# A PEER decoder block: expert gates written once to device memory as a table, instead of made anew for every chunk of expert rows

## The chip, the core and the metric

The kernel runs on one core of a Trainium2 chip. The metric is the device time of one launch in microseconds (us). Its engines appear in the rows as PE (TensorE), PEld (TensorE's weight loads), DVE (VectorE), ACT (ScalarE), POOL (GpSimd) and SP (SyncE, which here only issues transfers).

## What is computed

A decoder block over 256 tokens of width 2048: a token mixer (sparse attention and pooling), then a retrieval over 16384 single-neuron experts, which is the part that the change touches. Each token has 8 heads; each head picks 16 experts, and an expert's number is a pair of keys, first and second, each of 128. The reference, cut to this part:

```python
s_top, i_top = lax.top_k(sub, PEER_TOPK)
cand = s_top[..., 0, :, None] + s_top[..., 1, None, :]
cand_idx = i_top[..., 0, :, None] * PEER_KEYS + i_top[..., 1, None, :]
...
best, pos = lax.top_k(cand, PEER_TOPK)
experts = jnp.take_along_axis(cand_idx, pos, axis=-1)
gates = jax.nn.softmax(best, axis=-1)
...
    u = peer_u[ec]
    a = jax.nn.gelu(jnp.einsum('cd,ced->ce', hc, u, ...), approximate=False)
    vv = peer_v[ec]
    return jnp.einsum('ce,ced->cd', (a * gc).astype(hc.dtype), vv)
```

The kernel doesn't gather. It computes the activations of all 16384 experts for all 256 tokens, multiplies them with a gate that is zero where a token hasn't picked the expert, and goes on through all rows of peer_v.

## The kernel before

**Rows and chunks.** The experts are 128 rows (first key) of 128 (second key, on the partitions). Four chunks of CH = 32 rows follow each other. `up(c, a, per_unit)` computes the activations of chunk c: for each of its 32 rows it loads 1 MB of peer_u into one of RAW = 4 buffers "raw" (`load`), splits each half into a rounded part wH on ScalarE (line 120) and the rest wL on VectorE (line 121), three buffers of each, and makes 48 products of 128x256 (`mm3`, lines 130 to 132: wH with hH, wH with hL, wL with hH). A row is thus two halves of 24 products, one for each wH and wL. ScalarE's gelu (line 741) writes the row into `a`. `down(c, a, ...)` takes `a` through peer_v in the same way. The order is up(0), up(1), down(0), down(1), up(2), up(3), down(2), down(3).

**Gates.** For a token, the 128 picks give a first key, a second key and a gate. The picks stand on the partitions, so the gates of a token are a product over its picks: second-key mask (128 picks x 128 keys, "o2") with first-key mask times gate ("o1", in two 16-bit parts q = 0 and 1). `g_pieces(a, c)` does this for the 32 first keys of chunk c alone: `gates_piece` makes the first-key masks of 32 tokens (lines 705 and 708), `mult_piece` the second-key masks of 2 x 8 tokens (line 717) and 32 products of 32 columns into a PSUM tile "gp" (line 722), and scales and multiplies them into `a` (line 726). This gives 512 products of 32 columns per chunk, and the second-key masks of all 256 tokens anew in each chunk.

**Order.** The small pieces stand in a list `side`; `run_side(n)` takes n of them. `step` takes one behind every row of up and every pair of rows of down. `pace(R_U)` puts in a reduction for the modulation (`ada`, line 136, with a load of its own into a raw buffer) behind every fourth row while some are left. In up(0) the side pieces are the top-16 searches and the decoding of both 128-token groups ("routing"); in up(1) the gates of chunk 0, in down(0) those of chunk 1, in up(3) and down(2) those of chunks 2 and 3. Each engine then works in a fixed order of its own, which the framework's scheduler makes; a buffer that is taken again waits for all who used it. "o1" of q = 0 has one buffer, of q = 1 two, "o2" two, "gp" two. All loads are issued by SP, in order.

Of the kernel before, what the change touches and what calls it, by code (L numbers as in the profile page):

```python
# [9 lines left out]
F32 = mybir.dt.float32  # L10
F32R = mybir.dt.float32r
F16 = mybir.dt.float16
U32 = mybir.dt.uint32
AF = mybir.ActivationFunctionType
ALU = mybir.AluOpType
# [4 lines left out]
P = 128  # L20
T = 256
D = 2048
# [6 lines left out]
CH = 32  # L29
KGROUPS = ((0, 4), (4, 10), (10, 16))  # L30
NGU = 43
RAW = 4
R_K, R_Y, R_GA, R_WO, R_PQ, R_U = 0.6, 0.4, 0.7, 0.6, 0.3, 0.25
TB = 8
GATE_SCALE = 2.0 ** 15


@with_exitstack
def kernel(
# [22 lines left out]
    nc = tc.nc  # L62
    wgrp_in = (wgrp0_in, wgrp1_in, wgrp2_in)
    dve, act, pe = nc.vector, nc.scalar, nc.tensor
# [3 lines left out]
    stream = ctx.enter_context(tc.tile_pool(name="stream", bufs=3))  # L68
# [96 lines left out]
    def run_side(n):  # L165
        for _ in range(n):
            if side:
                side.pop(0)()
# [462 lines left out]
    def top_list(t, h):  # L631
        for s in range(2):
            l = 2 * h + s
            top16(stop_[t][:, l], itop[t][:, l], sub[l][:, t])

    def top_cand(t, h):
        l = 2 * h
        cand = px.tile([P, 16, 16], F32, name="cand", bufs=1)
        dve.tensor_tensor(cand, stop_[t][:, l, :, None].to_broadcast([P, 16, 16]),
                          stop_[t][:, l + 1, None, :].to_broadcast([P, 16, 16]), ALU.add)  # L640
        top16(best[:, h], pos[:, h], cand.rearrange("p a b -> p (a b)"))
# [24 lines left out]
    def decode_flip(t, s):  # L666
        ps = gps.tile([P, 512], F32, name="gp")[:, :P]
        pe.transpose(ps, late["sel", t, s], ident)
        act.copy(idxT[s][:, P * t:P * t + P], ps)

    def gates_of(t):
        e = px.tile([P, 8, 16], F32, name="cand", bufs=1)
        sm = px.tile([P, 8, 2], F32, name="gsm", bufs=2)
        dve.tensor_tensor(e, best, best[:, :, 0:1].to_broadcast([P, 8, 16]), ALU.subtract)
        act.activation(e, e, AF.Exp)
        dve.tensor_reduce(sm[:, :, 0:1], e, axis=AX.X, op=ALU.add)
        dve.reciprocal(sm[:, :, 1:2], sm[:, :, 0:1])
        dve.tensor_tensor(e, e, sm[:, :, 1:2].to_broadcast([P, 8, 16]), ALU.mult)
        late["e", t] = e
# [8 lines left out]
    def new_a(c):  # L688
        if c % 2 == 0:
            return [px.tile([P, ND, T], F32, name=f"r{i}") for i in (2, 3)]  # L690
        return [main.tile([P, ND, T], F32, name="r1"), px.tile([P, ND, T], F32, name="r4")]

    def g_pieces(a, c):
        o1_of = {}

        def gates_piece(grp):
            t0 = 32 * grp
            o1 = [px.tile([P, 32 // TB, CH, TB], F16, name=f"o1{q}", bufs=1 + q) for q in range(2)]
            o1_of[grp] = o1

            def per_token(src):
                return (src[:, t0:t0 + 32].rearrange("p (g t) -> p g t", t=TB)[:, :, None, :]
                        .to_broadcast([P, 32 // TB, CH, TB]))

            dve.tensor_tensor(o1[1], iota2[:, None, CH * c:CH * c + CH, :].to_broadcast([P, 32 // TB, CH, TB]),
                              per_token(idxT[0]), ALU.is_equal)
            for q in range(2):
                dve.tensor_tensor(o1[q], o1[1], per_token(gT[q]), ALU.mult)

        def mult_piece(b):  # L710
            t0 = 16 * b
            o1 = o1_of[b // 2]
            ps = gps.tile([P, 512], F32, name="gp")
            for x in range(16 // TB):
                t1 = t0 + TB * x
                o2 = px.tile([P, P, TB], F16, name="o2", bufs=2)
                dve.tensor_tensor(o2, iota2, idxT[1][:, None, t1:t1 + TB].to_broadcast([P, P, TB]), ALU.is_equal)  # L717
                g = (t1 % 32) // TB
                for i in range(TB):
                    k = CH * (TB * x + i)  # L720
                    for q in range(2):
                        pe.matmul(ps[:, k:k + CH], o2[:, :, i], o1[q][:, g, :, i], start=q == 0, stop=q == 1)  # L722
            v = ps.rearrange("p (t i) -> p i t", i=CH)
            for k in range(2):
                av = a[k][:, :, t0:t0 + 16]
                dve.scalar_tensor_tensor(av, v[:, 16 * k:16 * k + 16], 1.0 / GATE_SCALE, av,  # L726
                                         op0=ALU.mult, op1=ALU.mult)

        out = []
        for grp in range(8):  # L730
            out.append(lambda grp=grp: gates_piece(grp))
            out += [lambda b=b: mult_piece(b) for b in (2 * grp, 2 * grp + 1)]
        return out

    def up(c, a, per_unit):
        for e in range(CH):
# [32 lines left out]
                    k = 8 * hf + j - 1  # L769
                    nc.sync.dma_start(out=out[:, k:k + 2, :], in_=xT[:, k:k + 2, :])  # L770

    for t in range(2):
        for h in range(8):
            if t:
                side.append(lambda t=t, h=h: top_list(t, h))
            side.append(lambda t=t, h=h: top_cand(t, h))
        side.append(lambda t=t: decode(t, 0))
        side.append(lambda t=t: (decode_flip(t, 0), decode(t, 1)))
        side.append(lambda t=t: (decode_flip(t, 1), gates_of(t)))
        side.append(lambda t=t: gates_flip(t))  # L780

    def step(e):
        run_side(1)
        pace(R_U)

    a0 = new_a(0)
# [100 lines left out]
```

## Time and profile before

| | |
|---|---|
| three runs | 2384.88, 2385.82 (median), 2390.25 us |
| span of the profiled execution, first to last instruction | 2378.8 us |
| the median beyond that span | 7.0 us |
| PE, DVE, ACT busy, share of the span | 98%, 69%, 42% |
| up(0), first to last gelu | 771.23 to 962.16 us |
| up(1) | 966.56 to 1177.61 us |
| up(2) | 1581.04 to 1759.60 us |
| up(3) | 1765.36 to 1976.40 us |

The profiled execution's own time is its span; what a run takes beyond it lies before the first and after the last instruction. Busy shares are means over the whole; what bounds a stage is read in that stage, from the rests of its busiest engine and from what ended them.

### The profile page before, as it was taken

Reading aid. Unit: us, or ns where it says so; the run is one execution under the profiler, and the core shown is the slowest. Engines: PE = TensorE matmul, PEld = TensorE weight load, DVE = VectorE, ACT = ScalarE, POOL = GpSimd, SP = SyncE. Lnnn points to the kernel's source line nnn. Section 1 sums busy time; section 2 is a strip of 40 time slices with the busy share of each in tenths; the row PEclk is TensorE's granted clock in tenths of the full one; section 3 lists DMA queues with packets and bytes.
Section 4 is the critical chain, followed back from the end, with each engine's and each line's share of the span. In section 5 each row is a group of like instructions: output and inputs, shape, how many; then the busy total and the mean of one; then the engine's idle time right before and its main releaser. Section 6 shows DMA issues by size and latency. Waiting matters only on the chain.

```text
span 2378.8 us, 46564 instructions
## 1 busy us (share of the span) xinstructions
PE 2329.5 (98%) x19824; PEld 2288.2 (96%) x19824; DVE 1639.2 (69%) x2611; ACT 1002.9 (42%) x1479; POOL 4.8 (0%) x11
## 2 busy tenths in 40 slices
PE   6999999999999999999999999999999999999999
PEld 5899988999899899999999999999999999999999
DVE  7888977688777997665577655554445656675555
ACT  4544433744344343433433444444433333334443
POOL 0000000000000000000000000000000000000000
PEclk8999999999999999999999999999999999999999
DMA  8988866688755466544544455555554444445563
GB/s 341 333 312 315 312 232 234 247 322 303 291 188 205 178 237 224 207 167 145 176 151 150 160 179 177 195 188 185 179 177 146 156 160 160 144 158 169 187 201 119
DMA packets 88049, 494.04 MB, mean 208 GB/s; under 512 B 7913, under 2 KB 8961, under 8 KB 49441
## 3 DMA queue, kind: packets, MB, share of 16 engines
q1 hardware_dynamic: 87698, 490.90, 58.3%
q8 instruction: 155, 2.54, 0.4%
q14 instruction: 52, 0.43, 0.0%
q0 software_dynamic: 144, 0.17, 0.0%
HBM read 488.93 MB, written 2.11 MB: 206 GB/s over the span
## 4 chain that ended last, share of the span: by engine, by line
PE 87%; DVE 7%; DMA 4%; issue 1%; ACT 1%; SPq 0%; DVEq 0%; ACTq 0%
PE acc L130 26%; PE acc L132 26%; PE acc L131 26%; PE gp L722 5%; DMA raw<-in_ada_dram 3%; PE acc L503 2%; DVE wL L121 2%; DVE raw L136 2%; DVE o L660 1%; ACT wH L120 0%; PE mps L593 0%; DMA raw<-in_wgrp_dram 0%; PE mps L549 0%; PE mps L407 0%; PE mps L393 0%
## 5 line engine op out<-in xcount | busy, mean ns | idle before, releaser
L120 ACT CAST wH<-raw 128x1024 fp32r<-128x1024 f32 (+2 forms) x738 | 753.3, 1022 | 1229.0 <-PE acc L131 1167.3
L121 DVE TENSOR_TENSOR wL<-raw,wH 128x1024 fp32r<-128x1024 f32 (+2 forms) x738 | 874.3, 1188 | 526.8 <-ACT wH L120 525.4
L130 PE MATMUL acc<-hH,wH 128*128 128x256 f32 x3248 | 928.2, 286 | 19.7 <-ACT wH L120 18.2
L132 PE MATMUL acc<-hH,wL 128*128 128x256 f32 x3248 | 921.1, 284 | 6.1 <-DVE wL L121 5.9
L131 PE MATMUL acc<-hL,wH 128*128 128x256 f32 x3248 | 921.9, 284 | 0.1
L130 PEld LDWEIGHTS acc<-hH,wH 128*128 128x128 f32 x3248 | 626.7, 193 | 23.9 <-ACT wH L120 21.1
L132 PEld LDWEIGHTS acc<-hH,wL 128*128 128x128 f32 x3248 | 624.7, 193 | 9.2 <-DVE wL L121 9.0
L131 PEld LDWEIGHTS acc<-hL,wH 128*128 128x128 f32 x3248 | 626.1, 193 | 0.7 <-DVE hL L567 0.3
L130 PE MATMUL acc<-aH,wH 128*128 128x256 f32 x2048 | 577.4, 283 | 0.0
L132 PE MATMUL acc<-aH,wL 128*128 128x256 f32 x2048 | 576.8, 282 | 0.0
L131 PE MATMUL acc<-aL,wH 128*128 128x256 f32 x2048 | 576.6, 282 | 0.0
L130 PEld LDWEIGHTS acc<-aH,wH 128*128 128x128 f32 x2048 | 386.1, 189 | 0.0
L132 PEld LDWEIGHTS acc<-aH,wL 128*128 128x128 f32 x2048 | 385.9, 188 | 0.0
L131 PEld LDWEIGHTS acc<-aL,wH 128*128 128x128 f32 x2048 | 385.8, 188 | 0.0
L136 DVE CUSTOM_DVE_ANT_0 raw<-raw,cb 128x2048 f32<-128x2048 f32 x96 | 219.5, 2287 | 24.4 <-DMA raw<-in_ada_dram 24.2
L717 DVE TENSOR_TENSOR o<-iota,idxT 128x1024 f16<-128x1024 f16 x128 | 88.0, 688 | 92.4 <-PE gp L722 92.4
L722 PE MATMUL gp<-o,o 128*128 128x32 f16 x2048 | 137.7, 239 | 0.0
L722 PEld LDWEIGHTS <-o 128*128 128x128 f16 x2048 | 129.5, 163 | 2.9
L759 DVE TENSOR_TENSOR aL<-r,aH 128x256 fp32r<-128x256 f32 x256 | 107.0, 419 | 0.0
L758 ACT CAST aH<-r 128x256 fp32r<-128x256 f32 x256 | 102.2, 401 | 2.4 <-DVE r L726 2.4
L131 PE MATMUL acc<-m,wH 128*128 128x256 f32 x256 | 71.9, 282 | 0.0
L726 DVE SCALAR_TENSOR_TENSOR r<-gp,r 128x256 f32<-128x256 f32 x128 | 48.4, 420 | 21.5 <-PE gp L722 21.5
(207 smaller groups left out, 1397.5 us busy)
## 6 DMA issues: line engine op xcount, KB each, us to landing
raw<-in_u_dram SPq DMA_DIRECT2D x128, 1024.0 KB, 4.8
raw<-in_v_dram SPq DMA_DIRECT2D x128, 1024.0 KB, 5.1
raw<-in_ada_dram SPq DMA_DIRECT2D x96, 1024.0 KB, 5.5
raw<-in_wgrp_dram SPq DMA_DIRECT2D x43, 768.0 KB, 6.0
raw<-in_ybr_dram SPq DMA_DIRECT2D x16, 1024.0 KB, 6.0
raw<-in_wga_dram SPq DMA_DIRECT2D x16, 1024.0 KB, 4.9
raw<-in_wout_dram SPq DMA_DIRECT2D x16, 1024.0 KB, 4.8
raw<-in_wpq_dram SPq DMA_DIRECT2D x16, 1024.0 KB, 6.2
```

Source lines behind the costliest of these rows:

```text
L120: act.copy(wH[:, :n], src)
L121: dve.tensor_tensor(wL[:, :n], src, wH[:, :n], ALU.subtract)
L130: pe.matmul(ps, wH, xH, start=start, stop=False, **kw)
L131: pe.matmul(ps, wH, xL, start=False, stop=False, **kw)
L132: pe.matmul(ps, wL, xH, start=False, stop=stop, **kw)
L136: dve.tensor_tensor_reduce(raw, raw, cb, scale=1.0, scalar=0.0, op0=ALU.mult, op1=ALU.add, accum_out=modr[:, i:i + 1])
L503: pe.matmul(ps, ybr[0][:, o:o + P], pooled[k], start=k == 0, stop=k == 7)
L717: dve.tensor_tensor(o2, iota2, idxT[1][:, None, t1:t1 + TB].to_broadcast([P, P, TB]), ALU.is_equal)
L722: pe.matmul(ps[:, k:k + CH], o2[:, :, i], o1[q][:, g, :, i], start=q == 0, stop=q == 1)
L726: dve.scalar_tensor_tensor(av, v[:, 16 * k:16 * k + 16], 1.0 / GATE_SCALE, av, op0=ALU.mult, op1=ALU.mult)
L758: act.copy(aH, src)
L759: dve.tensor_tensor(aL, src, aH, ALU.subtract)
```

## The change

The gates of all 128 first keys are made once. `gates_build(x)`, x = 0 to 31, takes 8 tokens: both masks over all 128 keys (lines 705 and 706 of the changed kernel), two multiplications with the gate parts (708), 16 products of 128 columns (715) into two "gp" tiles, and two scalings on ScalarE (718) into "gstage", which is one of the four raw buffers. After every second build GpSimd's queue writes the stage, 1 MB, to a table "gdram" in device memory (722). The builds stand in `side` between the routing pieces, and `step` takes R_G = 1.1 pieces per row, so that they run in up(0) and up(1). `gates_apply(a, c, z)`, four per chunk, loads the chunk's 32 first keys of 64 tokens from the table (727), 1 MB in runs of 512 bytes, into a raw buffer, and multiplies `a` with them in two operations of 128x1024 (730). Lines above the change are one higher than before: wH 121, wL 122, the reduction 137.

```diff
--- before.py
+++ after.py
@@ -32,6 +32,7 @@
 RAW = 4
 R_K, R_Y, R_GA, R_WO, R_PQ, R_U = 0.6, 0.4, 0.7, 0.6, 0.3, 0.25
 TB = 8
+R_G = 1.1
 GATE_SCALE = 2.0 ** 15
 
 
@@ -690,47 +691,46 @@
             return [px.tile([P, ND, T], F32, name=f"r{i}") for i in (2, 3)]
         return [main.tile([P, ND, T], F32, name="r1"), px.tile([P, ND, T], F32, name="r4")]
 
+    gdram = dram.tile([P, 64, P, 4], F32, name="gdram")
+    gstage = {}
+
+    def gates_build(x):
+        t1 = TB * x
+        o2 = px.tile([P, P, TB], F16, name="o2", bufs=2)
+        o1 = [px.tile([P, P, TB], F16, name=f"o1{q}", bufs=1 + q) for q in range(2)]
+
+        def per_token(src):
+            return src[:, None, t1:t1 + TB].to_broadcast([P, P, TB])
+
+        dve.tensor_tensor(o2, iota2, per_token(idxT[1]), ALU.is_equal)
+        dve.tensor_tensor(o1[1], iota2, per_token(idxT[0]), ALU.is_equal)
+        for q in range(2):
+            dve.tensor_tensor(o1[q], o1[1], per_token(gT[q]), ALU.mult)
+        if x % 2 == 0:
+            gstage[0] = stream.tile([P, D], F32, name="raw", bufs=RAW)
+        for y in range(2):
+            ps = gps.tile([P, 512], F32, name="gp")
+            for i in range(4):
+                for q in range(2):
+                    pe.matmul(ps[:, P * i:P * i + P], o2[:, :, 4 * y + i], o1[q][:, :, 4 * y + i],
+                              start=q == 0, stop=q == 1)
+            n = 2 * (x % 2) + y
+            act.mul(gstage[0][:, 512 * n:512 * n + 512].rearrange("p (i t) -> p i t", t=4),
+                    ps.rearrange("p (t i) -> p i t", i=P), 1.0 / GATE_SCALE)
+        if x % 2 == 1:
+            g = 2 * (x - 1)
+            nc.gpsimd.dma_start(out=gdram[:, g:g + 4].rearrange("p g i t -> p (g i t)"), in_=gstage[0])
+
+    def gates_apply(a, c, z):
+        raw = stream.tile([P, D], F32, name="raw", bufs=RAW)
+        raw = raw.rearrange("p (g i t) -> p g i t", g=16, t=4)
+        nc.sync.dma_start(out=raw, in_=gdram[:, 16 * z:16 * z + 16, CH * c:CH * c + CH])
+        for k in range(2):
+            av = a[k][:, :, 64 * z:64 * z + 64].rearrange("p i (g t) -> p i g t", t=4)
+            dve.tensor_tensor(av, av, raw[:, :, 16 * k:16 * k + 16].rearrange("p g i t -> p i g t"), ALU.mult)
+
     def g_pieces(a, c):
-        o1_of = {}
-
-        def gates_piece(grp):
-            t0 = 32 * grp
-            o1 = [px.tile([P, 32 // TB, CH, TB], F16, name=f"o1{q}", bufs=1 + q) for q in range(2)]
-            o1_of[grp] = o1
-
-            def per_token(src):
-                return (src[:, t0:t0 + 32].rearrange("p (g t) -> p g t", t=TB)[:, :, None, :]
-                        .to_broadcast([P, 32 // TB, CH, TB]))
-
-            dve.tensor_tensor(o1[1], iota2[:, None, CH * c:CH * c + CH, :].to_broadcast([P, 32 // TB, CH, TB]),
-                              per_token(idxT[0]), ALU.is_equal)
-            for q in range(2):
-                dve.tensor_tensor(o1[q], o1[1], per_token(gT[q]), ALU.mult)
-
-        def mult_piece(b):
-            t0 = 16 * b
-            o1 = o1_of[b // 2]
-            ps = gps.tile([P, 512], F32, name="gp")
-            for x in range(16 // TB):
-                t1 = t0 + TB * x
-                o2 = px.tile([P, P, TB], F16, name="o2", bufs=2)
-                dve.tensor_tensor(o2, iota2, idxT[1][:, None, t1:t1 + TB].to_broadcast([P, P, TB]), ALU.is_equal)
-                g = (t1 % 32) // TB
-                for i in range(TB):
-                    k = CH * (TB * x + i)
-                    for q in range(2):
-                        pe.matmul(ps[:, k:k + CH], o2[:, :, i], o1[q][:, g, :, i], start=q == 0, stop=q == 1)
-            v = ps.rearrange("p (t i) -> p i t", i=CH)
-            for k in range(2):
-                av = a[k][:, :, t0:t0 + 16]
-                dve.scalar_tensor_tensor(av, v[:, 16 * k:16 * k + 16], 1.0 / GATE_SCALE, av,
-                                         op0=ALU.mult, op1=ALU.mult)
-
-        out = []
-        for grp in range(8):
-            out.append(lambda grp=grp: gates_piece(grp))
-            out += [lambda b=b: mult_piece(b) for b in (2 * grp, 2 * grp + 1)]
-        return out
+        return [lambda z=z: gates_apply(a, c, z) for z in range(4)]
 
     def up(c, a, per_unit):
         for e in range(CH):
@@ -769,18 +769,31 @@
                     k = 8 * hf + j - 1
                     nc.sync.dma_start(out=out[:, k:k + 2, :], in_=xT[:, k:k + 2, :])
 
-    for t in range(2):
+    def routing(t):
+        todo = []
         for h in range(8):
             if t:
-                side.append(lambda t=t, h=h: top_list(t, h))
-            side.append(lambda t=t, h=h: top_cand(t, h))
-        side.append(lambda t=t: decode(t, 0))
-        side.append(lambda t=t: (decode_flip(t, 0), decode(t, 1)))
-        side.append(lambda t=t: (decode_flip(t, 1), gates_of(t)))
-        side.append(lambda t=t: gates_flip(t))
+                todo.append(lambda h=h: top_list(t, h))
+            todo.append(lambda h=h: top_cand(t, h))
+        todo.append(lambda: decode(t, 0))
+        todo.append(lambda: (decode_flip(t, 0), decode(t, 1)))
+        todo.append(lambda: (decode_flip(t, 1), gates_of(t)))
+        todo.append(lambda: gates_flip(t))
+        return todo
+
+    build = [lambda x=x: gates_build(x) for x in range(32)]
+    side += routing(0)
+    later = routing(1)
+    for x in range(16):
+        side += [later.pop(0), build[x]]
+    side += later + build[16:]
+
+    owed = [0.0]
 
     def step(e):
-        run_side(1)
+        owed[0] += R_G
+        run_side(int(owed[0]))
+        owed[0] -= int(owed[0])
         pace(R_U)
 
     a0 = new_a(0)
```

Three places of the order. First VectorE in up(0), before the row whose halves are 26 and 27: the end of three builds (o_9517 and o_9518 are o1 of the third, o_9675 and o_9676 of a fourth; in names o1[0] is the output that reads gT_8291, o1[1] the one that reads gT_8292).

```order
L708 TENSOR_TENSOR o_9517<-o_9518,gT_8291 128x1024
L705 TENSOR_TENSOR o_9674<-iota_8293,idxT_8290 128x1024
L708 TENSOR_TENSOR o_9518<-o_9518,gT_8292 128x1024
L137 ISA raw,modr<-raw,cb 128x2048
L137 ISA modr 128x1
L706 TENSOR_TENSOR o_9676<-iota_8293,idxT_8289 128x1024
L705 TENSOR_TENSOR o_9772<-iota_8293,idxT_8290 128x1024
L708 TENSOR_TENSOR o_9675<-o_9676,gT_8291 128x1024
L122 TENSOR_TENSOR wL<-raw,wH 128x1024 x2
```

The reduction over 2048 columns and three operations of the next builds now stand between the third build's last multiplication and the next two wL.

Second, VectorE in up(1), before of chunk 0's gates and now of builds 28 to 31 (o_12767, o_12855, o_12943, o_13031 are o1[0], one buffer; o_12854, o_12942, o_13030 are o2). Before:

```order
L717 TENSOR_TENSOR o_10757<-iota_8293,idxT_8290 128x1024
L717 TENSOR_TENSOR o_10775<-iota_8293,idxT_8290 128x1024
L121 TENSOR_TENSOR wL<-raw,wH 128x1024 x2
L717 TENSOR_TENSOR o_10921<-iota_8293,idxT_8290 128x1024
L726 SCALAR_TENSOR_TENSOR r_8295<-gp,r_8295 128x16x16
L726 SCALAR_TENSOR_TENSOR r_8296<-gp,r_8296 128x16x16
L708 TENSOR_TENSOR o_10855<-o_10856,gT_8291 128x1024
L121 TENSOR_TENSOR wL<-raw,wH 128x1024
```

Now:

```order
L708 TENSOR_TENSOR o_12768<-o_12768,gT_8292 128x1024
L706 TENSOR_TENSOR o_12856<-iota_8293,idxT_8289 128x1024
L708 TENSOR_TENSOR o_12855<-o_12856,gT_8291 128x1024
L705 TENSOR_TENSOR o_12942<-iota_8293,idxT_8290 128x1024
L708 TENSOR_TENSOR o_12856<-o_12856,gT_8292 128x1024
L706 TENSOR_TENSOR o_12944<-iota_8293,idxT_8289 128x1024
L708 TENSOR_TENSOR o_12943<-o_12944,gT_8291 128x1024
L705 TENSOR_TENSOR o_13030<-iota_8293,idxT_8290 128x1024
L708 TENSOR_TENSOR o_12944<-o_12944,gT_8292 128x1024
L706 TENSOR_TENSOR o_13032<-iota_8293,idxT_8289 128x1024
L122 TENSOR_TENSOR wL<-raw,wH 128x1024 x2
```

Where wL stood between a few gate operations, three builds now stand without a wL between them, and each o1[0] is written in front of the next build's o2 and the own o1[1]. TensorE at the same place, the end of build 28 and the beginning of build 29:

```order
L715 MATMUL gp<-o_12767,o_12766 128x128
L715 LDWEIGHTS o_12766
L715 MATMUL gp<-o_12768,o_12766 128x128
L715 LDWEIGHTS o_12854
L715 MATMUL gp<-o_12855,o_12854 128x128
L715 LDWEIGHTS o_12854
L715 MATMUL gp<-o_12855,o_12854 128x128
L715 LDWEIGHTS o_12854
L715 MATMUL gp<-o_12856,o_12854 128x128
```

No weight product stands between the two builds.

Third, SP's queue at the end of up(1). Before:

```order
L113 DMA raw<-in_u_dram 128x2048 x19
L749 DMA raw<-in_v_dram 128x2x1024 x64
L113 DMA raw<-in_u_dram 128x2048 x64
L749 DMA raw<-in_v_dram 128x2x1024 x52
L770 DMA out_dram<-xT 128x512 x4
```

Now:

```order
L114 DMA raw<-in_u_dram 128x2048 x15
L727 DMA raw<-gdram 128x16x128 x2
L114 DMA raw<-in_u_dram 128x2048
L727 DMA raw<-gdram 128x16x128
L114 DMA raw<-in_u_dram 128x2048
L727 DMA raw<-gdram 128x16x128
L114 DMA raw<-in_u_dram 128x2048 x2
L749 DMA raw<-in_v_dram 128x2x1024
L727 DMA raw<-gdram 128x16x128
L749 DMA raw<-in_v_dram 128x2x1024
L727 DMA raw<-gdram 128x16x128
```

The table's reads stand among the last rows of peer_u and the first of peer_v; two rows stand behind the fourth read.

## Rows read from the trace of the kernel before

**Rows 1.** The page, parts 1 and 2: busy time, granted clock, GB/s by slice.

```profile
PE 2329.5 (98%) x19824; PEld 2288.2 (96%) x19824; DVE 1639.2 (69%) x2611; ACT 1002.9 (42%) x1479; POOL 4.8 (0%) x11
...
PEclk8999999999999999999999999999999999999999
...
GB/s 341 333 312 315 312 232 234 247 322 303 291 188 205 178 237 224 207 167 145 176 151 150 160 179 177 195 188 185 179 177 146 156 160 160 144 158 169 187 201 119
```

**Rows 2.** The page, part 4: the chain that ended last, by line.

```profile
PE acc L130 26%; PE acc L132 26%; PE acc L131 26%; PE gp L722 5%; DMA raw<-in_ada_dram 3%; PE acc L503 2%; DVE wL L121 2%; DVE raw L136 2%; DVE o L660 1%; ACT wH L120 0%; PE mps L593 0%; DMA raw<-in_wgrp_dram 0%; PE mps L549 0%; PE mps L407
```

**Rows 3.** Windows (us, PE, PEld, DVE, ACT, POOL, PEclk, DMA, GB/s): three stretches.

```profile
765.00:962.00 197.00, 189.22 (x1546) 187.74 (x1546) 182.14 (x404) 83.74 (x107) 0.00 (x0) 0.98 0.59 212
966.00:1177.00 211.00, 211.00 (x2002) 210.31 (x2001) 129.11 (x160) 74.73 (x97) 0.00 (x0) 1.00 0.48 170
1581.00:1760.00 179.00, 179.00 (x1494) 179.00 (x1493) 76.25 (x63) 74.17 (x95) 0.00 (x0) 1.00 0.52 183
```

**Rows 4.** Timeline of ACT (start us, us, what): first and last gelu, up(2), up(3).

```profile
1581.04 0.38 ACT L741 ACTIVATE r<-acc 128x256 f32<-128x256 f32 x1
...
1759.60 0.38 ACT L741 ACTIVATE r<-acc 128x256 f32<-128x256 f32 x1
...
1765.36 0.38 ACT L741 ACTIVATE r<-acc 128x256 f32<-128x256 f32 x1
...
1976.40 0.38 ACT L741 ACTIVATE r<-acc 128x256 f32<-128x256 f32 x1
```

**Rows 5.** Timeline of PE in up(1): one group of 32 gate products.

```profile
971.17 0.28 PE L132 MATMUL acc<-hH,wL 128*128 128x256 f32 x1
971.29 2.14 PE L722 MATMUL gp<-o,o 128*128 128x32 f16 x32
973.25 0.36 PE L130 MATMUL acc<-hH,wH 128*128 128x256 f32 x1
```

**Rows 6.** Chain, 674 to 765 us: the 128x128 float32 products.

```profile
679.88 0.45 PE mps L593 x4
```

**Rows 7.** Timeline of DVE at the same place in up(1).

```profile
970.72 2.28 DVE L136 CUSTOM_DVE_ANT_0 raw<-raw,cb 128x2048 f32<-128x2048 f32 x1
...
973.47 0.76 DVE L726 SCALAR_TENSOR_TENSOR r<-gp,r 128x256 f32<-128x256 f32 x2 [0.46 <-PE gp L722]
974.14 1.28 DVE L717 TENSOR_TENSOR o<-iota,idxT 128x1024 f16<-128x1024 f16 x2
975.34 1.22 DVE L121 TENSOR_TENSOR wL<-raw,wH 128x1024 fp32r<-128x1024 f32 x1
```

**Rows 8.** Timeline of PE in up(0): a rest before a product with wL.

```profile
899.90 0.39 PE L132 MATMUL acc<-hH,wL 128*128 128x256 f32 x1 [1.14 <-DVE wL L121]
900.12 0.28 PE L130 MATMUL acc<-hH,wH 128*128 128x256 f32 x1
900.24 0.28 PE L131 MATMUL acc<-hL,wH 128*128 128x256 f32 x1
```

**Rows 9.** Timeline of DVE at the same place.

```profile
898.63 1.22 DVE L121 TENSOR_TENSOR wL<-raw,wH 128x1024 fp32r<-128x1024 f32 x1
```

**Rows 10.** Lines by form, ACT: the cast, and a copy from PSUM.

```profile
L120 ACT CAST wH<-raw 128x1024 fp32r<-128x1024 f32 x645 | 676.4, 1049 | 1125.2 <-PE acc L131 1092.9 <-DMA raw<-in_wga_dram 19.1 <-issue 6.1
...
L594 ACT COPY r<-mps 128x256 f32<-128x256 f32 x16 | 6.0, 376 | 0.5 <-PE mps L593 0.5
```

**Rows 11.** DMA issues (KB each, median us from issue to landing).

```profile
raw<-in_u_dram SPq DMA_DIRECT2D x128, 1024.0 KB, 4.8
...
raw<-fd SPq DMA_DIRECT2D x1, 1024.0 KB, 7.8
...
fd<-pT POOLq DMA_DIRECT2D x1, 12.0 KB, 5.3
```

**Rows 12.** Timeline of PE in up(0): the longest rest.

```profile
820.10 0.45 PE L668 MATMUL gp<-ident,cand 128*128 128x128 f32 x1 [4.83 <-issue]
```

**Rows 13.** Windows, the time after that rest (columns as in rows 3).

```profile
818.80:825.60 6.80, 5.29 (x23) 5.03 (x24) 6.80 (x9) 0.27 (x1) 0.00 (x0) 0.50 0.36 108
```


## Prediction

> **What bounds the kernel now.** I began with the busy shares: TensorE works 98% of the span at a granted clock that stands at the top in every slice but the first [rows 1]. The chain that ended last says the same: 78% of the span is the three weight products, 5% the gate products of line 722 [rows 2]. So time taken from TensorE should come off the span, as long as nothing else becomes late where it was taken. That is read by stage. In up(1) (966 to 1177) and up(2) (1581 to 1760) TensorE never rests; in up(0) (765 to 962) it is busy 189.2 of 197 us and VectorE 182.1 [rows 3]. The change puts work into up(0) and up(1), and up(0) is where VectorE has 15 us free; up(1) has 82.
>
> The sum is made on the profiled execution: its span is 2378.8 us, and the median of the three runs lies 7.0 above it. I keep that distance.
>
> **Removed from TensorE.** up(2) and up(3) are the same loop without and with a chunk's gates. From first gelu to last, up(2) takes 1759.60 - 1581.04 = 178.56 us and up(3) 1976.40 - 1765.36 = 211.04 [rows 4]. So the 512 products of a chunk cost 32.5 us. As a check, one group of 32 takes from 971.29 to 973.25, 61 ns each [rows 5], which makes 31.4. Four chunks: **-130 us**. I take all of it as path: in up(1), where one chunk's products run now, the next busiest engine is at 61% (129.1 of 211 us) [rows 3].
>
> **Added to TensorE.** 512 products with 128 columns. The trace has none in 16 bits. Below stand the 61 ns of a product with the same weights and 32 columns [rows 5], and half of the 120 ns at which the 256-column products follow each other (971.17, 971.29) [rows 5]. Above stand the 128x128 float32 products of line 593, 0.45 us for four, 112 ns each [rows 6]. I take 62, since both lower rows share something with the new form, the one its weights, the other its columns per ns: **+32 us**. The upper end is +57. The Trainium skill's page TensorE: Matmul & The Clock Gate, section Back-to-back issue gap, gives about 81 ns for a sustained pair of weight load and product at N=128, which would make +41 and the whole 10 us worse; no row here shows that form, and the row for 32 columns already lies below it.
>
> **VectorE, ScalarE.** VectorE loses 96 o2 masks and 128 scalings and gains 32 long multiplications, ScalarE gains 64 scalings from PSUM. A mask costs 0.60 (two start 1.20 apart), a scaling 0.34, a float32 multiplication over 1024 columns 1.22, of which the next operation's early start takes 0.08, so 1.14 [rows 7], a ScalarE scaling of 512 columns about 0.6, as 256 cost 0.38 [rows 10]. The sum on VectorE is a loss of 64 us, but hidden behind TensorE before and after, so counted at nothing. The cover is that weights are ready ahead; where the order takes that away it counts, and that is the next part.
>
> **The bunches.** The order of the changed program doesn't spread the 32 builds. Counting half units of 24 weight products (2.88 us) from the start of up(0), eight times three builds stand back to back on TensorE (before halves 26, 40, 56, 70, 90, 98, 104 and 112), and the other eight alone. Within a bunch o1[0] has one buffer: its next multiplication waits for the last product of the build before, and behind it on VectorE stand the next mask and the other multiplication, which TensorE needs as well. So TensorE rests: from its last product to VectorE about 0.22 (the group ends near 973.25, line 726 begins at 973.47 [rows 5, 7]), 0.60 + 0.60 + 0.69 for three operations [rows 7], 0.05 back (a wL that ends at 899.85 releases the product at 899.90 [rows 8, 9]): 2.15 us. Sixteen builds follow another: 16 x 2.15 = **+34.4**. (Two of the sixteen products need only the first multiplication and go ahead; 0.12 that I leave out.)
>
> After the third build the next half needs its wL: one mask 0.60 and 1.22 for wL [rows 7] stand before it, of which the build's own 1.0 us and the weight products that need no wL cover all but 0.55: six bunches, +3.3. In the first bunch VectorE also has a modulation reduction of 2.2 [rows 7] and three more build operations there: 3.9. Before half 90 it has that and one more mask, 4.5. After the bunches at 40 and 56 a reduction with four build operations stands between two wL, longer than the half that covers it: +1.3 and +1.2. In all **+48.6** with the 34.4. To bound it: if VectorE's operations were hidden as they are now, 0; if each follow-on took 0.4 more, 55.
>
> One more wait is in the slots. The table stage of builds 10 and 11 takes the raw slot of builds 8 and 9, so ScalarE's scaling of build 10 waits until that write has landed, with the cast of half 58 behind it. Let the write take T. From the end of build 9 TensorE has a rest, build 10 and halves 56 and 57 (2.15 + 1.0 + 0.55 + 5.76 = 9.5); the write starts 1.0 after that end, and two scalings (1.2) and the cast (1.05) [rows 10] follow it: a rest of T - 6.2. For T the nearest row is a 12 KB store by the same queue, 5.3 us [rows 11]; 1 MB at the highest rate of a slice, 341 GB/s [rows 1], takes 3.1 more. T = 8.4; the wait is 2.2, of which 1.2 is counted above: **+1.0**.
>
> **Transfers.** 16 MB are written and 16 read beside the 494 MB of now; behind the writes on GpSimd's queue stands nothing but the next write. With T = 8.4 the row loads that wait on SP for a table slot have room: from the last build of a pair to the half that needs the row, less load 4.8 [rows 11], cast 1.05 [rows 10] and wL 1.22, there remain 10.5 us at three rows (21, 47, 50) and 12.4 at two (55, 59). Counted at nothing. At the end of up(1) the fourth piece of the table can be read only when the last write has landed, and SP has rows 62 and 63 queued behind it, VectorE the wL of half 124. From the start of build 31: 1.0 and 1.2 for products and scalings, T 8.4, the read 7.8 as the one load in 1 KB runs [rows 11] (these runs have 512 B), 2.3 and 1.0 for VectorE, 1.22 for wL: 22.9. TensorE comes to half 124 after 1.0 + 6 x 2.88 = 18.3. **+4.5**, bounds 0 and 8.
>
> **The clock.** After the 4.83 us of rest at 815 to 820 [rows 12] the granted clock stands at 0.50, 1.2 of 2.4 GHz, until 825.6: 23 products take 5.3 us that take 2.8 at the upper level, 2.5 lost [rows 13]; after the rest of 1.14 at 899 the products go on at 0.12 spacing [rows 8]. Two of the new rests come near the first, so **+5.0**; bounds 0 and what the clock rival below says.
>
> What up(0) loses today to the routing of the second 128 tokens is spread into up(1); its rests besides the 4.83 were 3.0 us (7.8 idle in all [rows 3]), a gain I leave to the range.
>
> **Sum:** -130 + 32 + 48.6 + 1.0 + 5.0 + 4.5 = -39. From 2378.8 that is a span of 2340, and **2347 us** by the median's distance. With its terms at their nearer bounds the case runs from 2325 to 2365.
>
> **Rivals.**
> - *The bunches cost nothing.* For it: up(1) has 82 us of VectorE free and TensorE's queue has nothing else to wait for. Against: the one buffer of o1[0] is a true wait. -130 + 32 + 4.5: 2292.
> - *The products with 128 columns go at 112 ns.* For it only line 593, which is float32. +25: 2372.
> - *The clock falls in every bunch.* For it: a bunch is 8 us in which TensorE works 3. Against: the rest of 1.14 did nothing to it. Eight bunches lose 2.5 each on weight products, and two builds in each 1.0: 36, less the 5.0 counted: 2378.
> - *The writes land late, and it is slower than before.* The writes come from GpSimd's queue while VectorE is busiest. Every us beyond the room stops TensorE at the three rows with 10.5, the two with 12.4, at build 10 and at the end of up(1): 3(T - 10.5) + 2(T - 12.4) + 2(T - 8.4) = 7T - 73. At T = 20 that is +67: 2414. It decides from T = 16.8, where the time stands 0.2% above the one before. For it: no 1 MB transfer by that queue is in the trace, and 5.3 us for 12 KB is slow. Against: the one store of that queue landed in 5.3 us [rows 11], under a third of 16.8. The Trainium skill's page SBUF — State Buffer, the box on the "DVE blocks DMA" trap, says that GpSimd cannot write its descriptors while VectorE runs an operation in a two-port mode. The masks look like such a mode (0.68 us for as many elements as wL takes 1.22 for [rows 7]); no run here shows what a write loses to it.
>
> **How the numbers follow.** The forecast 0.60, bunches free 0.10, 112 ns 0.07, clock 0.13, late writes 0.08, and 0.02 for a move that none of these name. Measured times of this kernel tell a difference over 0.2% (4.8 us) from none. The forecast, the free bunches and 112 ns are faster; of the clock's 2378, with some us to either side, a third lies above 2381. Faster 0.86, same 0.06, slower 0.08. The range leaves out the late writes and half of the free bunches: 2302 to 2386; the likeliest case alone is 2325 to 2365.
>
> **What would show it.** up(2) and up(3) both at 178 to 180 us from first gelu to last, down(0) and down(2) shorter by some 32 each. In up(0) and up(1) eight places with two rests of 2 us between builds, released by VectorE's multiplications; builds of 1.0 us. Writes of 8 to 9 us. A rest of some 4 us before half 124 released by a wL behind the table's read. The forecast is wrong if the weight loads on SP wait for table writes in many places, if the clock row shows 5 or 6 over several slices of up(1), or if builds take over 1.5 us at full clock.

## The result, and the profile after

| | before | changed |
|---|---|---|
| median of four runs | 2388.03 us | 2424.71 us (2421.52 to 2426.39) |
| ratio | | 1.0154, 95% interval 1.0139 to 1.0168 |
| span of the profiled execution | 2378.8 us | 2419.4 us |

Slower by 1.5%, where 39 us less were forecast. The profiled run of the changed kernel took 2421.52 us in all, 2.1 over its span; so most of the 7.0 us that the table ahead puts before the first and after the last instruction is a difference between executions. Busy time and clock of the changed kernel, from the page:

```profile
PE 2345.7 (97%) x18288; PEld 2255.2 (93%) x18288; DVE 1571.9 (65%) x2419; ACT 1038.8 (43%) x1543; POOL 13.3 (1%) x27
...
PEclk8999999999999988888889999999999999999999
```

TensorE issues 1536 products fewer and is busy 16 us longer than in [rows 1], and the granted clock shows 8 in place of 9 tenths over seven slices. The same windows as in [rows 3], by stage (us, PE, PEld, DVE, ACT, POOL, PEclk, DMA share, GB/s):

```profile
769.00:1027.00 258.00, 243.14 (x1728) 223.25 (x1727) 196.16 (x435) 94.14 (x126) 3.24 (x6) 0.89 0.50 180
1032.00:1318.00 286.00, 270.88 (x1820) 238.28 (x1819) 154.75 (x174) 101.98 (x143) 5.31 (x10) 0.86 0.52 181
1688.00:1867.00 179.00, 179.00 (x1494) 179.00 (x1493) 78.25 (x64) 74.16 (x95) 0.00 (x0) 1.00 0.55 183
```

And the gelus of the changed kernel, from the timeline of ACT: the first of up(0), the last of up(1), the first and last of up(2) and of up(3).

```profile
775.51 0.38 ACT L741 ACTIVATE r<-acc 128x256 f32<-128x256 f32 x1
...
1318.03 0.38 ACT L741 ACTIVATE r<-acc 128x256 f32<-128x256 f32 x1
...
1688.33 0.38 ACT L741 ACTIVATE r<-acc 128x256 f32<-128x256 f32 x1
...
1866.89 0.38 ACT L741 ACTIVATE r<-acc 128x256 f32<-128x256 f32 x1
...
1872.64 0.38 ACT L741 ACTIVATE r<-acc 128x256 f32<-128x256 f32 x1
...
2051.21 0.38 ACT L741 ACTIVATE r<-acc 128x256 f32<-128x256 f32 x1
```

What was to go has gone. up(3) takes 178.57 us where [rows 4] give 211.04; from the last gelu of up(1) to the first of up(2) it is 370.3 (403.4 before), from the last of up(3) to the end 368.2 (402.4): 32.5, 33.1 and 34.2 us less. The loss lies in up(0) and up(1): 542.5 us from first to last gelu, 406.4 before, +136.1 although chunk 0's old products (31 us) left as well. So the 32 builds cost about 167 us, where the forecast's terms gave 91. (The profiled executions differ by 40.6 us; 4.3 of these lie before the first gelu of up(0), which begins at 771.23 before and at 775.51 now. In the other runs it begins between 771.5 and 781.7, also where the kernel before was changed, so this says nothing of the builds.)

Here is the first bunch of three builds, timeline of PE in up(0):

```profile
850.75 3.94 PE L715 MATMUL gp<-o,o 128*128 128x128 f16 x16
855.25 0.67 PE L715 MATMUL gp<-o,o 128*128 128x128 f16 x2 [0.56 <-DVE o L708]
856.45 3.44 PE L715 MATMUL gp<-o,o 128*128 128x128 f16 x14 [0.53 <-DVE o L708]
860.45 0.67 PE L715 MATMUL gp<-o,o 128*128 128x128 f16 x2 [0.56 <-DVE o L708]
861.65 3.44 PE L715 MATMUL gp<-o,o 128*128 128x128 f16 x14 [0.53 <-DVE o L708]
864.73 0.57 PE L131 MATMUL acc<-hH,wH 128*128 128x256 f32 x1
865.10 0.42 PE L132 MATMUL acc<-hL,wH 128*128 128x256 f32 x1
867.61 0.58 PE L133 MATMUL acc<-hH,wL 128*128 128x256 f32 x1 [2.09 <-DVE wL L122]
```

The order and the releasers are the forecast ones: line 708 releases a build, wL releases the half behind the bunch. But a build of 16 products takes 3.5 us and not 1.0, and so the rests between builds are shorter than forecast (0.56 + 0.53, not 2.15), since VectorE works on while TensorE does. All waits of TensorE for these multiplications, in us, times and longest:

```profile
PE gp L715 <- DVE o L708: 18.9, 33, 1.4
```

The weight products behind follow each other at 0.21, where the upper clock gives 0.12. A build that stands alone shows both costs without any rest:

```profile
904.72 3.93 PE L715 MATMUL gp<-o,o 128*128 128x128 f16 x16
908.28 0.57 PE L131 MATMUL acc<-hH,wH 128*128 128x256 f32 x1
908.65 0.42 PE L132 MATMUL acc<-hL,wH 128*128 128x256 f32 x1
```

Its windows (columns as above): the build, the time behind it, and the next; last the greater part of the first bunch.

```profile
904.70:907.90 3.20, 3.20 (x16) 2.09 (x15) 3.06 (x11) 0.98 (x2) 0.00 (x0) 1.00 0.30 61
907.90:911.30 3.40, 3.40 (x18) 3.22 (x17) 3.16 (x7) 0.60 (x1) 0.54 (x1) 0.50 0.78 328
911.40:915.00 3.60, 3.60 (x33) 3.60 (x32) 1.59 (x6) 0.00 (x0) 0.00 (x0) 1.00 0.74 230
...
856.70:873.70 17.00, 13.81 (x60) 10.62 (x59) 12.63 (x23) 6.16 (x8) 0.58 (x1) 0.50 0.49 186
```

At the upper clock 15 steps from product to product take 3.5 us, 235 ns each; in the bunches they take 235 at either clock. TensorE is busy throughout, and still the clock is at 0.50 behind the build, with 18 products in 3.4 us where 33 fit into 3.6. Eight builds stand alone; behind five of them the clock falls so, behind three it stays up.

The transfers were quicker than forecast in the median, from the list of DMA issues. But of the 16 writes the last, for which the fourth read of chunk 0 waits on SP, took 9.8 us and not 4.1 (the third line is the same list between 1283 and 1284 us, the fourth SP's wait):

```profile
gdram<-raw POOLq DMA_DIRECT2D x16, 1024.0 KB, 4.1
raw<-gdram SPq DMA_DIRECT2D x16, 1024.0 KB, 6.8
...
gdram<-raw POOLq DMA_DIRECT2D x1, 1024.0 KB, 9.8
...
SPq L727 <- DMA gdram<-raw: 10.1, 1, 10.1
```

### The profile page after: what moved, and what is told of

It reads as the page before. It is cut to its first block, busy times and chain, and to the rows that moved or that the text cites. A ratio compares the mean times of both kernels' runs of the same rounds, so it can differ in the third digit from the quotient of the medians.

```text
span 2419.4 us, 43407 instructions
## 1 busy us (share of the span) xinstructions
PE 2345.7 (97%) x18288; PEld 2255.2 (93%) x18288; DVE 1571.9 (65%) x2419; ACT 1038.8 (43%) x1543; POOL 13.3 (1%) x27
## 4 chain that ended last, share of the span: by engine, by line
PE 87%; DVE 7%; DMA 3%; issue 1%; ACT 1%; DVEq 0%; ACTq 0%
PE acc L133 26%; PE acc L131 26%; PE acc L132 26%; PE gp L715 4%; PE acc L504 2%; DVE wL L122 2%; DVE raw L137 2%; DMA raw<-in_ada_dram 2%; DVE o L708 1%; DMA raw<-in_u_dram 1%; DMA raw<-in_wgrp_dram 1%; ACT wH L121 1%; PE mps L206 0%; DVE o L661 0%; PE mps L594 0%
## 5 line engine op out<-in xcount | busy, mean ns | idle before, releaser
L131 PE MATMUL acc<-hH,wH 128*128 128x256 f32 x3248 | 939.3, 290 | 21.4 <-ACT wH L121 19.7
L133 PE MATMUL acc<-hH,wL 128*128 128x256 f32 x3248 | 933.2, 288 | 9.2 <-DVE wL L122 9.1
L132 PE MATMUL acc<-hL,wH 128*128 128x256 f32 x3248 | 932.4, 287 | 0.1
L131 PEld LDWEIGHTS acc<-hH,wH 128*128 128x128 f32 x3248 | 636.8, 196 | 27.2 <-ACT wH L121 22.7
L132 PEld LDWEIGHTS acc<-hL,wH 128*128 128x128 f32 x3248 | 636.4, 196 | 0.8 <-DVE hL L568 0.3
L715 PE MATMUL gp<-o,o 128*128 128x128 f16 x512 | 130.4, 417 | 19.6 <-DVE o L708 18.9
L715 PEld LDWEIGHTS <-o 128*128 128x128 f16 x512 | 71.6, 148 | 67.8 <-DVE o L708 18.7
L708 DVE TENSOR_TENSOR o<-o,gT 128x1024 f16<-128x1024 f16 x64 | 44.1, 689 | 104.0 <-PE gp L715 103.9
L741 ACT ACTIVATE r<-acc 128x256 f32<-128x256 f32 x128 | 48.6, 380 | 73.0 <-PE acc L133 73.0
L718 ACT ACTIVATE raw<-gp 128x512 f32<-128x512 f32 x64 | 37.9, 598 | 95.9 <-PE gp L715 82.1
```

What stands on the lines that cost most here:

```text
L131: pe.matmul(ps, wH, xH, start=start, stop=False, **kw)
L132: pe.matmul(ps, wH, xL, start=False, stop=False, **kw)
L133: pe.matmul(ps, wL, xH, start=False, stop=stop, **kw)
L715: pe.matmul(ps[:, P * i:P * i + P], o2[:, :, 4 * y + i], o1[q][:, :, 4 * y + i], start=q == 0, stop=q == 1)
L741: act.activation(a[e // 16][:, e % 16], ps, AF.Gelu)
```

## The experiments

Three theories of the 235 ns. A: the moving operand. `o1[q][:, :, j]` takes every eighth 16-bit element, one in each 16 bytes, and 128 such columns take 1.83 ns each. B: the weights `o2[:, :, j]`, which have the same step. C: the form, any 16-bit product with 128 columns.

**Moving operand at step 1 (e1_mov1).**

```diff
-        o1 = [px.tile([P, P, TB], F16, name=f"o1{q}", bufs=1 + q) for q in range(2)]
+        o1 = [px.tile([P, TB, P, 1], F16, name=f"o1{q}", bufs=1 + q) for q in range(2)]
...
-   pe.matmul(..., o2[:, :, 4 * y + i], o1[q][:, :, 4 * y + i], ...)
+   pe.matmul(..., o2[:, 0, :, j], o1[q][:, j, :, 0], ...)
```

> Edit: o1 of gates_build laid out token by token, so that the moving operand of the 512 table products has step 1 element and not 8 (16 bytes); the weights o2 stay at step 8. Changed kernel: 235 ns per product at either clock, 2424.7 us. Theory A (the step of the moving operand sets the price, 1.83 ns a column): products at 55 to 80 ns, 512 x 165 = 85 us less on TensorE; the o1 operations have a broadcast as innermost dimension and may cost 1.1 instead of 0.6 us on VectorE, some 30 us back in the bunches: 2340 to 2385. Theory B (the step of the weights sets it): 235 ns stay, 2425 to 2460. Theory C (any 16-bit product with 128 columns costs this): 235 ns stay, 2425 to 2460.

2397.65 us, ratio to before 1.0038 [1.0025, 1.0051]. A lone build, timeline of PE:

```profile
905.95 1.18 PE L725 MATMUL gp<-o,o 128*128 128x128 f16 x16
906.94 0.36 PE L131 MATMUL acc<-hH,wH 128*128 128x256 f32 x1
```

1.0 us for 16, 64 ns each from product to product (most steps are 60 ns, one is 113): A holds for the price, B and C fall. The time came down by 27 only and missed the 2340 to 2385. The o1 operations cost VectorE 1.22 us each and not 0.69, and TensorE waits for two of them between the builds of a bunch, 45.8 us in all where it was 18.9. The multiplications of this run (times, busy us, mean ns):

```profile
L717 DVE TENSOR_TENSOR o<-o,gT 128x1024 f16<-128x1024 f16 x64 | 78.1, 1221 | 74.0 <-PE gp L725 73.9
```

**Weights at step 1 (e2_wgt1).** The same edit on o2, with o1 as it was.

```diff
-        o2 = px.tile([P, P, TB], F16, name="o2", bufs=2)
+        o2 = px.tile([P, TB, P, 1], F16, name="o2", bufs=2)
```

> Edit: o2 laid out token by token, so that the weights have step 1; the moving operand stays at step 8. A: 235 ns stay, 2425 to 2445. B: products at 55 to 80 ns, 2340 to 2370. C: 235 ns stay.

2427.91 us in one run. A lone build:

```profile
908.48 3.79 PE L725 MATMUL gp<-o,o 128*128 128x128 f16 x16
911.90 0.48 PE L131 MATMUL acc<-hH,wH 128*128 128x256 f32 x1
```

225 ns each from product to product: B falls here too. The weights' step is worth 10 ns.

**Moving operand at steps 2 and 4 (e3_mov2, e5_mov4).** o1 is laid out in groups of two or four tokens, which leaves the multiplications on VectorE at 0.69 us (lines at the end of this part).

```diff
-        o1 = [px.tile([P, P, TB], F16, name=f"o1{q}", bufs=1 + q) for q in range(2)]
+        o1 = [px.tile([P, TB // 2, P, 2], F16, name=f"o1{q}", bufs=1 + q) for q in range(2)]
```

> Edit: o1 laid out in pairs of tokens, so that the moving operand has step 2 elements (4 bytes); weights at step 8. A: if the price goes with the bytes that the operand spans, a quarter of 235, about 60 ns; if any step over one element costs the same, 235. B and C: 235 ns. Time 2340 to 2380 in the first case, 2420 to 2445 in the others.

> Edit: o1 in groups of four tokens, moving operand at step 4 elements (8 bytes); weights at step 8. Known: step 1 61 ns, step 2 62 to 65 ns, step 8 235 ns at the upper clock. If the price goes with the bytes that 128 columns span (235 ns for 2 KB): 118 ns, 2365 to 2390. If there is a limit only between 8 and 16 bytes: 62 to 65 ns, 2345 to 2360. If every step over 4 bytes costs the same: 235 ns, 2415 to 2435.

Step 2: 2354.01 us in one run, against 2386.77 before on the same chip. Step 4: 2370.07, also one run, against 2388.43. A lone build of each, step 2 first:

```profile
902.96 1.23 PE L721 MATMUL gp<-o,o 128*128 128x128 f16 x16
904.00 0.36 PE L131 MATMUL acc<-hH,wH 128*128 128x256 f32 x1
```

```profile
901.81 2.14 PE L721 MATMUL gp<-o,o 128*128 128x128 f16 x16
903.70 0.36 PE L131 MATMUL acc<-hH,wH 128*128 128x256 f32 x1
```

Steps of 1, 2, 4 and 8 elements cost 64, 67, 123 and 235 ns a product: nearly free up to 4 bytes, and from there with the bytes spanned. Behind all eight lone builds at step 2 the clock stays up, where at step 8 it fell behind five (window of the run with step 2, columns as above):

```profile
902.90:910.00 7.10, 7.10 (x68) 7.01 (x68) 6.93 (x18) 1.49 (x3) 0.54 (x1) 1.00 0.62 201
```

VectorE in the run with step 2: the multiplications (line 713) are as quick as before, but the first-key mask (711), which here reads the key numbers in runs of two out of eight, takes 1.11 us in place of 0.69; at step 4 both take 0.69. Last, TensorE's wait for the multiplications:

```profile
L713 DVE TENSOR_TENSOR o<-o,gT 128x1024 f16<-128x1024 f16 x64 | 44.1, 690 | 41.6 <-PE gp L721 40.8
...
L711 DVE TENSOR_TENSOR o<-iota,idxT 128x1024 f16<-128x1024 f16 x32 | 35.6, 1113 | 0.0
...
PE gp L721 <- DVE o L713: 28.7, 32, 2.7
```

**The kernel before with the moving operand at step 1 (e4_before_mov1).** If its 61 ns for 32 columns were 32 times 1.9, they must fall.

```diff
-            o1 = [px.tile([P, 32 // TB, CH, TB], F16, name=f"o1{q}", bufs=1 + q) for q in range(2)]
+            o1 = [px.tile([P, 32, CH], F16, name=f"o1{q}", bufs=1 + q) for q in range(2)]
```

> Edit: in the kernel before, o1 laid out token by token, so that its 2048 products of 32 columns read the moving operand at step 1. A: their 61 ns were 32 columns at 1.9 ns; they fall to what weight load and issue allow, 30 to 55 ns: 2048 x 6 to 31 ns = 12 to 63 us less, 2325 to 2376. B and C: 61 ns and 2388 stay (2385 to 2392).

2387.13 us, ratio 1.0001 [0.9989, 1.0013], a miss for A as I had put it.

```profile
974.49 2.12 PE L725 MATMUL gp<-o,o 128*128 128x32 f16 x32
976.46 0.36 PE L130 MATMUL acc<-hH,wH 128*128 128x256 f32 x1
```

62 ns each, as at step 8 in [rows 5]. With step 1 most products of 32 columns and most of 128 follow each other at the same 60 ns; at step 8, 32 columns at 1.83 ns (59 ns) lie just under that floor. The old form hid its step; the new one, with the same number of columns in all (2048 x 32 = 512 x 128), doesn't.

**Spreading the builds.** With the price settled, the rests and the clock were left. In two runs each build's products are queued behind the row before it, and its masks behind that row's last wL, at step 8 (e6_spread) and at step 2 (e8_mov2_spread).

```diff
-    build = [lambda x=x: gates_build(x) for x in range(32)]
+    def build_behind_row(x):
+        with tc.issue_after(last_product), tc.issue_after(last_wL):
+            gates_build(x)
+    build = [lambda x=x: build_behind_row(x) for x in range(32)]
```

> Edit: in the changed kernel every build's products are queued on TensorE behind the last product of the row before, and its VectorE operations behind that row's last wL, so that no two builds but one pair stand together; the moving step stays 8 elements. The product price is unchanged, 235 ns. Theory A as it stands (price +89, rests between builds +25, lower clock on weight products +22): the rests go, and the clock with them: 2424.7 - 47 = 2375 to 2390. Rival (the clock falls because the slow products themselves count as little work, not because of the rests): rests go, clock stays low for as long as before: 2395 to 2410. Rival (my forecast's error lay in the bunches and not in the price): under 2370.

> Edit: both together, moving step 2 and spread builds. Theory A: 512 products at 62 to 65 ns, no rests, clock up: -131 + 33 + about 5 at the end of up(1): 2285 to 2305. If rests and low clock of the run with step 2 alone came from elsewhere (VectorE late, slots): 2310 to 2354.

2480.65 us (1.0388 [1.0371, 1.0404]) and 2382.24 us (0.9987 [0.9974, 1.0001]): both worse than with the bunches, and no theory had it. On ScalarE a row's gelu, which waits for TensorE, now stood in front of the next row's first cast at every second build, and in up(0) and up(1) TensorE waited 18 times for a cast (27.9 and 29.5 us), in the changed kernel once. Two more runs, at step 2 (e9_mov2_woven) and 8 (e11_woven_step8), put a build into the middle of a row.

```diff
+        with tc.issue_after(first_wL_of_row):
+            o2, o1 = gates_masks(x)
...
+        with tc.issue_after(last_product_of_first_half), tc.issue_after(second_cast_of_row):
+            gates_products(x, o2, o1)
```

> Edit: moving step 2; a build's masks are queued on VectorE behind the first wL of a row, its products on TensorE behind the first half of that row, its scalings on ScalarE behind that row's second cast. The run with spread builds showed 1.8 to 2.0 us of rest before the first product of the next row and 1.0 before its third, since the scalings stood before the next cast on ScalarE. Theory (price 62 to 65 ns, rests are a matter of the order alone): no rests at the builds, clock at the upper level, -131 + 33, and 5 to 10 at the end of up(1), where the last build now comes 3 halves later: 2290 to 2310. Rival (the builds cost VectorE or the slots more than the rows can hide): rests move elsewhere, 2320 to 2360.

> Edit: the same order with the moving operand left at step 8. Theory (235 ns a product, and a build of 3.5 us alone lets the clock fall for 3.4 us behind it, as builds 3, 11 and 31 of the changed kernel did): against the run with step 2, 512 x 172 = +88 and 32 x 1.5 = +48 at most: 2400 to 2440. Rival (a build without rests leaves the clock up): +88 alone, 2380 to 2400.

2377.0 us (0.9961 [0.9948, 0.9975]) and 2477.24 us (1.038 [1.0352, 1.0408]). Both miss every range that was put up. The rests stayed: at step 2 TensorE rests 64 us in up(0) and up(1), 66 in the spread run at step 2. ACT and PE of the run at step 2 behind a row with a build:

```profile
1105.20 0.38 ACT L771 ACTIVATE r<-acc 128x256 f32<-128x256 f32 x1 [2.33 <-PE acc L136]
1105.48 2.93 ACT L124 CAST wH<-raw 128x1024 fp32r<-128x1024 f32 x3
```

```profile
1104.88 0.28 PE L136 MATMUL acc<-hH,wL 128*128 128x256 f32 x1
1106.57 0.38 PE L134 MATMUL acc<-hH,wH 128*128 128x256 f32 x1 [1.41 <-ACT wH L124]
```

The gelu waits for the row's last product, the cast for the gelu, the next row for the cast. The pair of runs still tells one thing: in the same order, step 8 costs 100 us more than step 2. In up(0) and up(1) of the two profiled runs it is 92 us: the gate products take 79 more, the weight products, more often at the lower clock, 24 more, and TensorE rests 11 less. Of the builds that TensorE makes in one piece and without a rest, the clock falls behind 11 of 21 at step 8 and behind none of 21 at step 2. One of the 11 (the run at step 8, the build and the time behind it):

```profile
874.70:879.10 4.40, 4.40 (x24) 3.06 (x23) 4.40 (x12) 2.00 (x3) 0.00 (x0) 1.00 0.44 140
879.20:882.60 3.40, 3.40 (x18) 3.40 (x18) 1.00 (x5) 0.15 (x1) 0.58 (x1) 0.50 0.90 371
```

**Casts ahead (e12_ahead).** The weights of a row are split ahead of the row before, and its gelu is queued behind the next row's second cast:

```diff
+            w = weights(e + 1, masks_of_next_build)
             for d in range(ND):
                 mm3(ps, now[d // 8], ...)
-            act.activation(a[e // 16][:, e % 16], ps, AF.Gelu)
+            with tc.issue_after(last_cast):
+                act.activation(a[e // 16][:, e % 16], ps, AF.Gelu)
```

> Edit: moving step 2; the weights of a row are loaded and split ahead of the row before, so that on ScalarE a row's gelu stands behind the next row's second cast; a build's masks are queued on VectorE between that next row's two wL, its products on TensorE behind the row. In both spread orders tried so far ScalarE had a row's gelu, which waits for TensorE, in front of the next row's first cast, at every second build: 1.7 us of rest and 1.0 behind it. Theory (the rests between rows come from that order on ScalarE, and the low clock from the rests): no rest at the builds but for up(0)'s top-16 work, clock at the upper level; 2386.8 - 131 + 33 and some 10 at the end of up(1): 2290 to 2315. Rival (a build costs a rest wherever it stands, by the raw slot that its stage takes): 2340 to 2380.

2335.55 us, ratio 0.9790 [0.9777, 0.9803]: faster than both kernels, though 20 us over the upper end. The rests at the builds are nearly gone; what TensorE waited for in up(0) and up(1) of this run (waits: us in total, times, longest):

```profile
PE acc L134 <- ACT wH L124: 17.6, 4, 7.8
PE acc L136 <- DVE wL L125: 10.7, 9, 2.6
PE gp L673 <- DVE cand L668: 6.4, 2, 3.2
PE gp L736 <- DVE o L725: 3.2, 10, 0.6
```

Builds wait 3.2 us in all (18.9 in the changed kernel). The edit also moved the masks, so it isn't shown that the casts alone did it; what is shown is that the waits for casts, 18 and 19 in the spread orders, came down to 4. Most of the first row are two rests of 7.5 and 7.8 at the end of up(1), before halves whose row of peer_u stands on SP behind a table read. The last run (e13_late_read) moves the fourth read of chunk 0 behind up(1) and starts the builds earlier.

```diff
-R_G = 1.1
+R_G = 1.2
...
-    side += g_pieces(a0, 0)
+    first = g_pieces(a0, 0)
+    side += first[:3]
     up(1, a1, step)
...
+    side += first[3:]
     run_side(len(side))
```

> Edit to the run e12_ahead: R_G 1.2, and the fourth piece of the table for chunk 0 is read and applied behind up(1), with no row of peer_u queued on SP behind it. e12_ahead has two rests of 7.8 and 8.1 us at the end of up(1), before halves that wait for a row load which stands on SP behind a table read, and behind each the clock is at 0.50 for 10.2 us. Theory (the handover's cost is that order on SP): both rests go, 16 us and some 9 of low clock, of which one shorter rest of 3 to 6 us comes back before down(0): 2310 to 2322. Rival (the read's landing itself holds up(1)'s end wherever it stands): 2330 to 2345.

2340.54 us, ratio 0.9803 [0.9782, 0.9825], no difference to the run before, and inside the rival's range. One of the two rests went, the other is 5.7 us, and up(1) took 232 us in place of 239, but up(0), where R_G 1.2 packs more into a full VectorE, 218 in place of 209. Two things were changed at once, so this run doesn't settle the end of up(1).

## Why the prediction was wrong, step by step

**The step that failed** is "Added to TensorE": "I take 62, since both lower rows share something with the new form, the one its weights, the other its columns per ns: +32 us." The products measured 235 ns, 120 us in all, +88 over the term and twice the upper bound of 112. With the moving operand at step 2 the price is 67 ns and the time 2354, so this term, with what it does to the clock, carries most of the 78 us between forecast and result. The rows I used had either few columns at step 8 (32, hidden under the floor of 60 ns) or many at step 1 (256, at 0.47 ns a column); the new form is the first with many columns at a wide step. The bound was in the row: 61 ns over 32 columns is 1.9 ns a column, which for 128 gives 244. I read 61 as a price per product and did not read it per column as well. That 244 comes so near is partly chance: at step 1 the 32 columns take 62 ns too, and 128 take 64. The 2048 products of 32 columns and the 512 of 128 move the same 65536 columns, and on TensorE the change exchanged 125 us for 120.

The Trainium skill, page SBUF — State Buffer, in a note of the section on the DMA port swizzle, says that consecutive accesses within one 16-byte line run at full rate and need at least two hits per line. The run at step 8, one 16-bit element per line, agrees; step 4, with two, does not, at 123 ns against 67. The 81 ns for a sustained pair at N=128 that the Trainium skill's page TensorE: Matmul & The Clock Gate gives in the section Back-to-back issue gap, and that I had weighed, is high for step 1 and 2 (64 and 67).

**Removed**: -130 forecast, 31 + 32.5 + 33.1 + 34.2 = 131 measured. Right.

**The bunches**: the mechanism was right, the places too; the size was +48.6, and the waits of TensorE for line 708 sum to 18.9 us, because a build of 3.5 us covers much of what VectorE does. With builds of 1.1 us (step 2) the same wait is 28.7, closer to the forecast 34.4.

**The clock**: +5.0 forecast for two rests. Between the first gelu of up(0) and the last of up(1), 246 weight products began at the lower clock, most of them 213 ns apart in place of 120, where 22 did before: +24 us. The clock fell in all eight bunches, which was the third rival, though not for its reason (in the first bunch TensorE rests 2.2 of 14 us), and, by no case of mine, behind five of the eight lone builds, which have no rest. At step 2 it stayed up behind those.

**Slots and end of up(1)**: 15 of the 16 writes took 4.1 to 4.8 us and not 8.4. So no rest came at build 10 (T under 6.2), and none at the row loads (SP waited five times for a write, 43.3 us in all, and TensorE for none of these). Before half 124 TensorE rested 1.4 + 0.8 in place of 4.5, first for ScalarE's wH and then for wL, but not because the write was quick: the one that counts there took 9.8, and the half's wL came 25.4 us after the start of build 31, where I had 22.9. TensorE itself came later, after 22.7 in place of 18.3, since the build took 3.6 and the clock fell behind it. Two errors met there. An estimate from the Trainium skill, page DMA: Bandwidth & Descriptors, section Anatomy of one DMA — SWDGE (gpsimd) path (2.0 us and 436 GB/s), gives 4.4 for 1 MB: it agrees with the 15, not with the last.

**The sum again**: -131 + 120 for the products, +22 for TensorE's rests in up(0) and up(1) (30.0 against 7.8) and +24 for the clock is +35, of a measured +37 in the medians. The run at step 2 takes 2354, 7 us from the forecast of 2347, but not term by term. In its up(0) and up(1) the gate products take 46 us where the forecast had 32 (a quarter of them at the lower clock), the rests grow by 35 where it had 54, and the lower clock costs 17 more where it had 5. So that nearness is in part luck.

**The rivals**: the 112 ns case pointed the right way and was less than half of it. The late writes, the only case on the slower side, did not happen: none took the 16.8 us at which that case decides. That the masks run in a two-port mode was a guess; what the runs show is that the first 15 writes kept to 4.1 to 4.8 us while VectorE was busy for two thirds of the time (363 of 561 us). My own sign for a wrong forecast, "builds take over 1.5 us at full clock", is the one that came.

## What to carry to other kernels

Read a product's time both per product and per column, and look at the step of its moving operand, before a form with other columns is priced from it: a floor can hide a rate. A layout made for VectorE (eight tokens innermost) is paid for on TensorE; here groups of two tokens cost TensorE next to nothing and VectorE only a slower mask (1.11 us in place of 0.69). When work is spread by hand over a static order, check every engine's order: putting the builds apart on TensorE and VectorE alone made the kernel slower; the order that was faster also put ScalarE's casts ahead of the gelu that waits.

## What the runs showed of the hardware

TensorE's clock can fall behind 3.5 us of products whose moving operand has a step of 16 bytes, with no rest anywhere (1.00 at 904.7 to 907.9, 0.50 to 911.3): it did so behind five of eight such builds in the changed kernel, and behind none of eight at step 2. Those slow products themselves cost 235 ns at either clock, and at step 4 123 ns at either; at step 1 and 2 they take 64 and 67 ns at the upper clock and 107 at the lower. VectorE multiplies 1024 16-bit elements in 0.69 us with pairs of tokens innermost, and in 1.22 with one token broadcast innermost.
